# Gathering the inputs of four experts at a time instead of eight, with a fifth slot in a weight ring and layer-norm rows spread on the core

## The chip, the cores and the metric

The kernel runs on one core of a Trainium2 chip. The metric is the device time of one execution in microseconds (us). Where several runs are shown, their median is meant.

## The reference

One decoder layer on 256 tokens of width 1024. A mixer (gated linear attention and causal pooling) comes first, then a layer norm, then a mixture of 64 experts of which every token uses 8, then a second layer norm. The part that the change touches is the mixture:

```python
def expert_block(args):
    xb, gb = args
    h = (jax.nn.silu(jnp.einsum('td,edf->tef', xb, w_exp_gate))
         * jnp.einsum('td,edf->tef', xb, w_exp_up))
    return jnp.einsum('tef,efd->td', h * gb[..., None], w_exp_down)
...
x <- LayerNorm(alpha * x + mix(x))        # first norm, rows ln1_g and ln1_b
x <- LayerNorm(alpha * x + moe(x))        # second norm
```

Each expert has three float32 matrices of 1 MB: gate and up (1024 x 256) and down (256 x 1024). All 64 experts are read, 192 MB.

## The kernel before, in words

**Weights.** All weight loads stand in one list, in the order of use, and `Ring` (L52) issues them on SyncE's queue, one tile of 1 MB (128 partitions x 8 KB) each. The tiles lie in slots: ring1 has 8, ring2 has 6, ring3 has 4 (`NR1, NR2, NR3`, L23), and two more take the place of the transposed input (xTh, xTl). A slot takes the next load of the list as soon as its last reader is done (`done`, L104). Ring3 is opened at L808, late in the mixer's output stage, in memory that the mixer has given back. It takes no new load after q = 4 and is released at q = 7, where the shared expert's tensors take its place.

**Gathered inputs.** Each expert has 32 slots (CAP) for each of two token tiles of 128. `build_p` (L882) writes, for a token tile, a 0/1 matrix P8 of 128 tokens x (8 experts x 32 slots) with one VectorE instruction. `gather` (L889) multiplies it with the normed input, which is held as the sum of two float32r tensors, xh and xl. For each of 8 channel groups k there are four matmuls (xh and xl of two token tiles), each with 128 x 128 weights of its own and 256 moving columns (L899). One PSUM bank holds the result of one k, and `affine` (L769 to L773) applies the norm's gain and offset while it is copied to SBUF, odd k on VectorE, even k on ScalarE. The copy, xg, holds eight experts, 16 KB of each partition.

**The expert loop** (L1177) takes four experts per step q, 16 steps. The order of TensorE's work in a step is written out: `gate_up` of the first pair, the transposes of the hidden layer (`hidden_t`), the scatter of finished outputs (`flush`), `slot_gates` (two matmuls with P8 as weights and 8 columns), `build_pt`, half of the down products of the step before (`downs`), `gate_up` of the second pair, transposes, scatter, then at odd q the gather for the next eight experts (`gather(q // 2 + 1)`, L1235), then the other half of the down products. The first gather is at L934, ahead of the loop. At q = 10 the shared expert's up product (L832, tile w_sh_up, which stands in the list behind the second pair of q = 10) is placed between `slot_gates` and `build_pt`, at q = 11 its down product (L965).

**Rows of the first norm.** `residual` (L969) adds the normed input to the output sums, by quarters c of the channels, at q = 2 to 5 (`RES`). For it `load_rows` (L984) loads a quarter of ln1_g and of ln1_b, each copied by the DMA to all 128 partitions (128 KB written each), for c = 0 and 1 at q = 0 and for c = 2 and 3 at q = 3 and 4 (`ROWS`).

Of the kernel before, what the change touches and what calls it, by code (L numbers as in the profile page):

```python
# [5 lines left out]
FT = mybir.dt.float32  # L6
FR = mybir.dt.float32r
# [3 lines left out]
OP = mybir.AluOpType  # L11
# [4 lines left out]
E, FF, CAP = 64, 256, 32  # L16
# [3 lines left out]
NEG = -1e30  # L20
SPLIT1, SPLIT2 = 2, 3

NR1, NR2, NR3 = 8, 6, 4  # L23
LENT = ("up", 3)
CLOSE3, SH_X2, SH_UP, SH_DOWN, TAIL = 7, 8, 10, 11, 12
ROWS, RES = {0: (0, 1), 3: (2,), 4: (3,)}, {2: 0, 3: 1, 4: 2, 5: 3}

C_ID, C_MASK, C_TRI, C_IOTA, C_RC, C_SLOT, C_OWN = 0, 128, 320, 448, 480, 544, 545
C_COLS = 549
# [80 lines left out]
def body(ctx, tc, A, out, dbg=lambda *a: None, stop=None):  # L110
    nc = tc.nc
    ctx.enter_context(tc.manual_schedule())
    PE, V, S, G = nc.tensor, nc.vector, nc.scalar, nc.gpsimd
# [81 lines left out]
    def bank(tag, shape, name):  # L195
        t = psum.tile([128, 512], FT, name=name, tag=tag, bufs=4)
        n = 1
        for s in shape:
            n *= s
        v = t[:, :n]  # L200
        if len(shape) == 2:
            v = v.rearrange("p (a b) -> p a b", b=shape[1])
        elif len(shape) == 3:
            v = v.rearrange("p (a b c) -> p a b c", b=shape[1], c=shape[2])
        return v
# [3 lines left out]
    iota = cst[:, C_IOTA:C_IOTA + CAP]  # L209
# [11 lines left out]
    R1 = keep.tile([128, 2, E], FT, name="R1")  # L221
# [29 lines left out]
    for n in range(2):  # L251
# [12 lines left out]
                                     ap=[[0, 128], [1, E]]))  # L264
# [53 lines left out]
    p = bank("a", (128,), "warm")  # L318
# [450 lines left out]
    def affine(k, dst, p, on_vector):  # L769
        if on_vector:  # L770
            V.tensor_scalar(dst, p, g1T[:, k:k + 1], b1T[:, k:k + 1], op0=OP.mult, op1=OP.add)  # L771
        else:
            S.activation(dst, p, AF.Identity, bias=b1T[:, k:k + 1], scale=g1T[:, k:k + 1])  # L773
# [21 lines left out]
    moe = tc.alloc_tile_pool(name="moe", bufs=1, reuse_waits="tile")  # L795
    xh = moe.tile([128, 2, 8, 128], FR, name="xh")
    xl = moe.tile([128, 2, 8, 128], FR, name="xl")
# [10 lines left out]
    ring3 = tc.alloc_tile_pool(name="ring3", bufs=NR3, reuse_waits="tile")  # L808
    ring.open(ring3, "w3", NR3)
    mid = tc.alloc_tile_pool(name="mid", bufs=1, reuse_waits="tile")  # L810
    early = moe.tile([128, 4096], FT, name="x2T", tag="xg", bufs=1)
    x2T = early[:, :8 * T].rearrange("p (k t) -> p k t", t=T)
    sc = mid.tile([128, 2, E], FT, name="sc")
    pscore = bank("a", (2, E), "pscore")
# [29 lines left out]
    mb, mr = mbr[:, 0], mbr[:, 1]  # L844
    sel = mid.tile([128, 2, E], FT, name="sel")
    selb = mid.tile([128, 2, E], BF, name="selb")
    P8 = {}

    def group_sums(t):

# [28 lines left out]
        PE.matmul(prank, trib, selb, start=True, stop=True)  # L879
        V.scalar_tensor_tensor(R1, prank, 1.0, selb, op0=OP.add, op1=OP.mult)  # L880

    def build_p(o, t):  # L882

        if t == 0:
            P8[o] = moe.tile([128, 2, 8, CAP], FR, name="P8", tag="P8", bufs=1)
        V.tensor_tensor(P8[o][:, t], iota[:, None, :].to_broadcast([128, 8, CAP]),
                        R1[:, t, 8 * o:8 * o + 8, None].to_broadcast([128, 8, CAP]), OP.is_equal)

    def gather(o, banks="b", at_once=1):  # L889


        parts = [(0, xh), (0, xl), (1, xh), (1, xl)]
        for k0 in range(0, 8, at_once):
            ks = range(k0, k0 + at_once)
            p = {k: bank(banks[k % len(banks)], (2, 8, CAP), "pgat") for k in ks}
            for some in (parts[:3], parts[3:]):
                for k in ks:
                    for t, part in some:
                        PE.matmul(p[k][:, t].rearrange("p e s -> p (e s)"), part[:, t, k],  # L899
                                  P8[o][:, t].rearrange("p e s -> p (e s)"), start=part is xh, stop=part is xl)  # L900
            for k in ks:
                affine(k, xg[:, k].rearrange("p e t s -> p t e s"), p[k], k % 2)

    G.tensor_copy(xh[:, 0], by_channel(0))
    G.tensor_sub(xl[:, 0], by_channel(0), xh[:, 0].bitcast(FT))
# [21 lines left out]
    S.activation(xh[:, 1], by_channel(1), AF.Copy)  # L927
    ring.issue(ring1, "w1", NR1)
    dbg("x2T", x2T)
    xg = moe.tile([128, 4096], FT, name="xg", tag="xg", bufs=1).rearrange("p (k e t s) -> p k e t s", e=8, t=2, s=CAP)  # L930
    for t in range(2):
        build_p(0, t)
    V.tensor_sub(xl[:, 1], by_channel(1), xh[:, 1].bitcast(FT))  # L933
# [48 lines left out]
    rows1 = {}  # L982

    def load_rows(c):  # L984

        for n in "gb":
            rows1[n, c] = rest.tile([128, 256], FT, name="row" + n, bufs=2)
            src = A["ln1_" + n]
            nc.sync.dma_start(rows1[n, c], bass.AP(tensor=src.tensor, offset=src.offset + 256 * c,
                                                   ap=[[0, 128], [1, 256]]))  # L990

    mid.release()
    rest = tc.alloc_tile_pool(name="rest", bufs=1, reuse_waits="tile")
    GS, PT, HT = {}, {}, {}

    def slot_gates(q):

        p = bank("b", (4, 4), "pgs")
        for t in range(2):
            lhsT = P8[q // 2][:, t, 4 * (q % 2):4 * (q % 2) + 4].rearrange("p e s -> p (e s)")  # L1000
            PE.matmul(p[:, 2 * t:2 * t + 2], lhsT, gates[:, t, :, 4 * q:4 * q + 4], start=True, stop=True)
        own = st1.rearrange("p t c n -> p (t c n)")[:, :16].rearrange("p (a b) -> p a b", b=4)
        GS[q] = moe.tile([128, 2], FT, name="gsl", bufs=2)
        V.tensor_mul(own, p, cst[:, None, C_OWN:C_OWN + 4].to_broadcast([128, 4, 4]))
        V.tensor_reduce(GS[q], own.rearrange("p (t h) e -> p t (h e)", t=2), axis=AX.X, op=OP.add)
# [12 lines left out]
    def gate_up(i):  # L1018
        p = bank("b", (2, FF), "pgu")
        for g, n in enumerate(("gate", "up")):  # L1020
            w = [ring.get(li[n, 2 * i + c]) for c in range(2)]
            for k in range(8):
                for c in range(2):
                    e = (2 * i + c) % 8
                    PE.matmul(p[64 * c:64 * c + 64, g], xg[:, k, e].rearrange("p t s -> p (t s)"),  # L1025
                              w[c][:, k], start=k == 0, stop=k == 7, tile_position=(0, 64 * c))
            for c in range(2):
                ring.done(li[n, 2 * i + c])
        sg = moe.tile([128, FF], FT, name="sg", tag="sg", bufs=1)
        h = moe.tile([128, FF], FT, name="h", tag="h", bufs=1)  # L1030
        S.activation(sg, p[:, 0], AF.Silu)  # L1031
        V.tensor_mul(h, sg, p[:, 1])  # L1032
        return h
# [127 lines left out]
    def flush(keep=0):  # L1161
        while len(ready) > keep:
            scatter(ready.pop(0))
# [12 lines left out]
    hb = None  # L1176
    for q in range(NQ):  # L1177
        last = q == NQ - 1
        for c in ROWS.get(q, ()):
            load_rows(c)  # L1180
        if q in RES:
            ready.append(residual(0, RES[q]))
        ha = gate_up(2 * q)
        if q:
            hidden_t(2 * q - 1, hb)
        flush()
        slot_gates(q)
        if q % 2 and not last:
            build_p(q // 2 + 1, 0)
            build_p(q // 2 + 1, 1)  # L1190
        if q in RES:
            ready.append(residual(1, RES[q]))
        if q == 7:
            rest.release()
        if q == CLOSE3 - 3:
            ring.closed.add("w3")
        if q == CLOSE3:
            ring3.release()
            overflow()
            shp = tc.alloc_tile_pool(name="shp", bufs=1, reuse_waits="tile")  # L1200
            SH["x2"] = shp.tile([128, 8, T], FT, name="x2")
            for t in range(2):
                SH[t] = shp.tile([128, 8, 128], FT, name=f"xn{t}")
                G.tensor_add(SH[t], xh[:, t].bitcast(FT), xl[:, t].bitcast(FT))
        if q == SH_X2:

            for t in range(2):
                to_x2(SH["x2"], transposes(SH[t]), t, (0, 1, 2, 3))
        if q == SH_UP:
            p = bank("b", (2, T), "shu")  # L1210
            shared_in("w_sh_up", p, SH["x2"], slice(0, T))
            ring.done(li["w_sh_up"])
            V.tensor_mul(SH["h"], SH["h"], p)
        if q == SH_DOWN:
            shared_down()
            shp.release()
        if q == TAIL:
            tail = tc.alloc_tile_pool(name="tail", bufs=1, reuse_waits="tile")
            lnr = tail.tile([1, 2, D], FT, name="lnr2")
            nc.sync.dma_start(lnr[:, 0], A["ln2_g"])  # L1220
            nc.sync.dma_start(lnr[:, 1], A["ln2_b"])
            g2 = tail.tile([128, D], FT, name="g2")
            b2 = tail.tile([128, D], FT, name="b2")
        if q == TAIL + 1:
            G.partition_broadcast(g2, lnr[:, 0])
            G.partition_broadcast(b2, lnr[:, 1])
        build_pt(q)
        cs = pieces_of(q - 1)
        if q and not last:
            downs(q - 1, cs[0])  # L1230
        hb = gate_up(2 * q + 1)
        hidden_t(2 * q, ha)
        flush()
        if q % 2 and not last:
            gather(q // 2 + 1)  # L1235
        if q and not last:
            downs(q - 1, cs[1])
            done_downs(q - 1)
# [12 lines left out]
    o = [tail.tile([128, D], FT, name=f"o{t}") for t in range(2)]  # L1251
# [54 lines left out]
```

## Time and profile before

| | us |
|---|---|
| median of three runs (712.38 to 715.11) | 714.49 |
| the profiled execution, its time | 714.68 |
| its span in the trace | 712.9 |
| TensorE busy | 675.9 |
| VectorE busy | 292.4 |
| ScalarE busy | 229.3 |

The span is what the trace shows from the first to the last instruction, and 1.8 us of the execution's time lie around it. A position in the trace is given as time from the start of the span. The mixer takes the first 218 us or so, the router and the first gather some 20 more, and the expert loop runs from 240 us to 700 us. Matmuls overlap in the engine: a row's duration is that of one from its start to its end, and the cost of a row of them is the distance between their starts.

### The profile page before, as it was taken

The page shows a single profiled execution, that of the slowest core. Times are in us where ns is not written, and L with a number is a line of the kernel's source. Part 1 is how long each engine was busy: PE and PEld are TensorE (multiplying, and loading weights), DVE is VectorE, ACT ScalarE, POOL GpSimd, SP SyncE. Part 2 cuts the span into 40 slices and gives each one's busy share as a digit, 9 for nine tenths or more (in the row PEclk, how much of TensorE's full clock was granted, in tenths as well). Part 3 has the DMA queues.
Part 4 walks back from the last instruction along what each step waited for, and adds up shares of the span by engine and source line. Part 5 has one row for each costly group of instructions (what it writes and reads, how often), then busy time and mean ns, then how long its engine had stood idle before and what let it go on. Part 6 is the DMA issues. An engine that isn't in the chain of part 4 may idle for free. (4 is left out here: it accounts for less than half of the span.)

```text
span 712.9 us, 13836 instructions
## 1 busy us (share of the span) xinstructions
PE 675.9 (95%) x6004; PEld 481.0 (67%) x6004; DVE 292.4 (41%) x480; ACT 229.3 (32%) x356; POOL 61.0 (9%) x51
## 2 busy tenths in 40 slices
PE   7999999999999799999999999997959999999993
PEld 7999999999999556556556546554544465565641
DVE  3589745946676313444444123311302131221126
ACT  3654645764444213123123113211201121121142
POOL 1053303600002000000000002000000000100001
PEclk8999999999999999999999999999979999999997
DMA  8995543499667699999999999999998999999981
GB/s 277 301 310 174 155 142 119 133 385 419 240 241 294 212 424 397 405 422 410 416 419 419 421 419 417 422 419 419 422 421 351 416 403 423 418 422 420 389 262 61
DMA packets 70068, 243.10 MB, mean 341 GB/s; under 512 B 7122, under 2 KB 41682, under 8 KB 46196
## 3 DMA queue, kind: packets, MB, share of 16 engines
q1 hardware_dynamic: 69860, 242.12, 87.1%
q8 instruction: 48, 0.79, 0.5%
q10 hardware_dynamic: 144, 0.07, 0.1%
q14 instruction: 16, 0.13, 0.1%
HBM read 241.11 MB, written 1.05 MB: 340 GB/s over the span
## 5 line engine op out<-in xcount | busy, mean ns | idle before, releaser
L1025 PE MATMUL pgu<-w,xg 128*64 128x256 f32 x1744 | 227.7, 385 | 8.0 <-DVE maxi L955 4.4
L1025 PEld LDWEIGHTS pgu<-w,xg 128*64 128x64 f32 x1744 | 141.8, 138 | 82.8 <-ACT Y L1055 10.1
L1050 PE MATMUL py<-w,ht 128*32 128x512 f32 (+1 forms) x1016 | 120.0, 558 | 0.4 <-ACT x L773 0.3
L287 DVE TENSOR_TENSOR sl<-w,sh 128x1024 fp32r<-128x1024 f32 (+1 forms) x63 | 80.3, 1281 | 43.8 <-ACT sh L286 43.6
L1032 DVE TENSOR_TENSOR h<-sg,pgu 128x256 f32<-128x256 f32 x32 | 13.5, 421 | 188.5 <-ACT sg L1031 157.8
L1056 DVE SCALAR_TENSOR_TENSOR Y<-py,gsl,Y 128x512 fp32r<-128x512 f32 (+1 forms) x70 | 48.9, 704 | 91.8 <-ACT Y L1055 91.8
L1055 ACT ACTIVATE Y<-py,gsl 128x512 fp32r<-128x512 f32 (+1 forms) x70 | 45.3, 650 | 120.7 <-PE py L1050 120.7
L290 PE MATMUL proj<-xTh,sh 128*128 128x256 f32 x288 | 83.8, 291 | 0.0
L292 PE MATMUL proj<-xTh,sl 128*128 128x256 f32 x288 | 82.1, 285 | 0.0
L291 PE MATMUL proj<-xTl,sh 128*128 128x256 f32 x288 | 81.7, 284 | 0.0
L1031 ACT ACTIVATE sg<-pgu 128x256 f32<-128x256 f32 x32 | 12.3, 385 | 200.8 <-PE pgu L1025 200.8
L286 ACT ACTIVATE sh<-w 128x1024 fp32r<-128x1024 f32 (+1 forms) x63 | 64.3, 1028 | 35.2 <-PE proj L292 13.4
L1050 PEld LDWEIGHTS py<-w,ht 128*32 128x32 f32 x1016 | 31.7, 109 | 47.5 <-issue 41.7
L290 PEld LDWEIGHTS proj<-xTh,sh 128*128 128x128 f32 x288 | 55.1, 191 | 0.6 <-issue 0.3
L291 PEld LDWEIGHTS proj<-xTl,sh 128*128 128x128 f32 x288 | 55.4, 192 | 0.1
L292 PEld LDWEIGHTS proj<-xTh,sl 128*128 128x128 f32 x288 | 54.9, 190 | 0.0
L1025 PE MATMUL pgu<-xTh,xg 128*64 128x256 f32 x208 | 47.7, 381 | 0.0
L1025 PEld LDWEIGHTS pgu<-xTh,xg 128*64 128x64 f32 x208 | 27.7, 137 | 16.6 <-DVE Y L1056 5.9
L1050 PE MATMUL py<-xTl,ht 128*32 128x512 f32 x80 | 36.2, 594 | 0.0
L771 DVE TENSOR_SCALAR xg<-pgat,cols_sb 128x512 f32<-128x512 f32 x32 | 25.7, 809 | 14.2 <-PE pgat L899 12.2
L899 PE MATMUL pgat<-P,xl 128*128 128x256 f32 x128 | 30.6, 283 | 0.5 <-DVE xl L933 0.5
L899 PE MATMUL pgat<-P,xh 128*128 128x256 f32 x128 | 30.4, 283 | 0.0
(269 smaller groups left out, 946.3 us busy)
## 6 DMA issues: line engine op xcount, KB each, us to landing
w<-in_w_exp_up SPq DMA_DIRECT2D x58, 1024.0 KB, 14.1
w<-in_w_exp_gate SPq DMA_DIRECT2D x51, 1024.0 KB, 15.0
w<-in_w_exp_down SPq DMA_DIRECT2D x51, 1024.0 KB, 19.7
w<-in_w_in SPq DMA_DIRECT2D x21, 1024.0 KB, 7.9
xTh<-in_w_exp_gate SPq DMA_DIRECT2D x9, 1024.0 KB, 15.9
w<-in_w_exp_down SPq DMA_DIRECT2D x22, 256.0 KB, 6.0
xTl<-in_w_exp_down SPq DMA_DIRECT2D x5, 1024.0 KB, 12.0
w<-in_w_gla_up SPq DMA_DIRECT2D x4, 1024.0 KB, 11.2
```

The costliest lines, as they stand in the source:

```text
L286: S.activation(hi, src, AF.Copy)
L287: eng.tensor_sub(lo, src, hi.bitcast(FT))
L290: PE.matmul(o, ah, bh, start=start, stop=False, skip_group_check=shared_bank)
L291: PE.matmul(o, ah, bl, start=False, stop=False, skip_group_check=shared_bank)
L292: PE.matmul(o, al, bh, start=False, stop=stop, skip_group_check=shared_bank)
L771: V.tensor_scalar(dst, p, g1T[:, k:k + 1], b1T[:, k:k + 1], op0=OP.mult, op1=OP.add)
L899: PE.matmul(p[k][:, t].rearrange("p e s -> p (e s)"), part[:, t, k], P8[o][:, t].rearrange("p e s -> p (e s)"), start=part is xh, stop=par ...
L1025: PE.matmul(p[64 * c:64 * c + 64, g], xg[:, k, e].rearrange("p t s -> p (t s)"), w[c][:, k], start=k == 0, stop=k == 7, tile_position=(0, ...
L1032: V.tensor_mul(h, sg, p[:, 1])
L1050: PE.matmul(p[32 * c:32 * c + 32], HT[2 * q + c // 2][:, j, c % 2, t], ring.get(li["down", 4 * q + c])[:, j, cs], start=j == 0, stop=j == ...
L1055: S.activation(hi, p, AF.Copy, scale=g)
L1056: V.scalar_tensor_tensor(lo, p, g, hi.bitcast(FT), op0=OP.mult, op1=OP.subtract)
```

## The change

Inputs are gathered for four experts, in every step q but the last, instead of for eight in every other one. P4 and xg are half as large. A gather still has 8 channel groups with four matmuls each, now with 128 moving columns; two channel groups share a PSUM bank. The memory given back goes to a fifth slot of ring3. The rows of the first norm are loaded onto one partition, for one quarter per step (q = 1 to 4), and GpSimd copies them to the other partitions with `partition_broadcast`.

```diff
-NR1, NR2, NR3 = 8, 6, 4
+NR1, NR2, NR3 = 8, 6, 5
-ROWS, RES = {0: (0, 1), 3: (2,), 4: (3,)}, {2: 0, 3: 1, 4: 2, 5: 3}
+ROWS, RES = {1: 0, 2: 1, 3: 2, 4: 3}, {2: 0, 3: 1, 4: 2, 5: 3}
...
-    early = moe.tile([128, 4096], FT, name="x2T", tag="xg", bufs=1)
+    early = moe.tile([128, 2048], FT, name="x2T", tag="xg", bufs=1)
...
-    def build_p(o, t):
+    def build_p(q, t):
         if t == 0:
-            P8[o] = moe.tile([128, 2, 8, CAP], FR, name="P8", tag="P8", bufs=1)
-        V.tensor_tensor(P8[o][:, t], iota[:, None, :].to_broadcast([128, 8, CAP]),
-                        R1[:, t, 8 * o:8 * o + 8, None].to_broadcast([128, 8, CAP]), OP.is_equal)
+            P4[q] = moe.tile([128, 2, 4, CAP], FR, name="P4", tag="P4", bufs=1)
+        V.tensor_tensor(P4[q][:, t], iota[:, None, :].to_broadcast([128, 4, CAP]),
+                        R1[:, t, 4 * q:4 * q + 4, None].to_broadcast([128, 4, CAP]), OP.is_equal)
-    def gather(o, banks="b", at_once=1):
+    def gather(q, banks="b", at_once=1):
         parts = [(0, xh), (0, xl), (1, xh), (1, xl)]
-        for k0 in range(0, 8, at_once):
-            ks = range(k0, k0 + at_once)
-            p = {k: bank(banks[k % len(banks)], (2, 8, CAP), "pgat") for k in ks}
+        rhs = [P4[q][:, t].rearrange("p e s -> p (e s)") for t in range(2)]
+        for k0 in range(0, 8, 2 * at_once):
+            ks = range(k0, k0 + 2 * at_once)
+            p = {k // 2: bank(banks[k // 2 % len(banks)], (2, 2, 4 * CAP), "pgat") for k in ks[::2]}
             for some in (parts[:3], parts[3:]):
                 for k in ks:
                     for t, part in some:
-                        PE.matmul(p[k][:, t].rearrange("p e s -> p (e s)"), part[:, t, k],
-                                  P8[o][:, t].rearrange("p e s -> p (e s)"), start=part is xh, stop=part is xl)
+                        PE.matmul(p[k // 2][:, k % 2, t], part[:, t, k], rhs[t], stop=part is xl,
+                                  start=k % 2 == 0 and t == 0 and part is xh, skip_group_check=True)
             for k in ks:
-                affine(k, xg[:, k].rearrange("p e t s -> p t e s"), p[k], k % 2)
+                affine(k, xg[:, k].rearrange("p e t s -> p t e s"),
+                       p[k // 2][:, k % 2].rearrange("p t (e s) -> p t e s", s=CAP), k % 2)
...
     def load_rows(c):
-        for n in "gb":
-            rows1[n, c] = rest.tile([128, 256], FT, name="row" + n, bufs=2)
-            src = A["ln1_" + n]
-            nc.sync.dma_start(rows1[n, c], bass.AP(tensor=src.tensor, offset=src.offset + 256 * c,
-                                                   ap=[[0, 128], [1, 256]]))
+        rows1["one"] = rest.tile([1, 2, 256], FT, name="rowone")
+        for i, n in enumerate("gb"):
+            nc.sync.dma_start(rows1["one"][:, i], A["ln1_" + n][:, 256 * c:256 * (c + 1)])
+
+    def spread_rows(c):
+        for i, n in enumerate("gb"):
+            rows1[n, c] = rest.tile([128, 256], FT, name="row" + n)
+            G.partition_broadcast(rows1[n, c], rows1["one"][:, i])
...
     for q in range(NQ):
-        for c in ROWS.get(q, ()):
-            load_rows(c)
+        if q in ROWS:
+            load_rows(ROWS[q])
...
-        if q % 2 and not last:
-            build_p(q // 2 + 1, 0)
-            build_p(q // 2 + 1, 1)
+        if not last:
+            build_p(q + 1, 0)
+            build_p(q + 1, 1)
...
         hidden_t(2 * q, ha)
         flush()
-        if q % 2 and not last:
-            gather(q // 2 + 1)
+        if q in ROWS:
+            spread_rows(ROWS[q])
+        if not last:
+            gather(q + 1)
```

`slot_gates` and `gate_up` read P4[q] and expert e % 4 of xg accordingly.

## Rows read from the trace of the kernel before

**Rows 1.** The page: busy time by engine; TensorE's granted clock (tenths) in 40 slices.

```profile
PE 675.9 (95%) x6004; PEld 481.0 (67%) x6004; DVE 292.4 (41%) x480; ACT 229.3 (32%) x356; POOL 61.0 (9%) x51
PEclk8999999999999999999999999999979999999997
```

**Rows 2.** Busy time by stretch; the columns stand in the first line.

```profile
core 0: us, PE busy (x) PEld busy (x) DVE busy (x) ACT busy (x) POOL busy (x), PEclk, DMA share, GB/s
283.00:286.00 3.00, 3.00 (x30) 1.43 (x24) 1.69 (x3) 0.92 (x2) 0.00 (x0) 1.00 0.71 227
286.00:480.00 194.00, 192.29 (x1683) 112.04 (x1679) 65.75 (x122) 47.83 (x86) 4.73 (x2) 1.00 1.01 418
515.00:535.00 20.00, 9.98 (x47) 8.00 (x49) 0.62 (x3) 0.00 (x0) 0.00 (x0) 0.74 1.01 421
535.00:700.00 165.00, 164.41 (x1466) 90.91 (x1458) 40.06 (x75) 36.92 (x66) 2.48 (x2) 1.00 0.95 378
```

**Rows 3.** Timeline of PE, 480 to 535: start, us, work, [idle before, releaser].

```profile
480.33 4.64 PE L1050 MATMUL py<-w,ht 128*32 128x512 f32 x32
...
492.82 5.11 PE L1025 MATMUL pgu<-w,xg 128*64 128x256 f32 x30 [2.81 <-DMA w<-in_w_exp_up]
497.86 0.50 PE L1039 MATMUL pht<-cst,h 128*128 128x128 f32 x2
...
525.24 9.45 PE L832 MATMUL shu<-x,w 128*128 128x256 f32 x32 [10.02 <-DMA w<-in_w_sh_up]
```

**Rows 4.** The chain that ended last, where nothing waits: start, us, work.

```profile
437.62 3.82 PE pgat L899 x32
441.44 3.57 PE py L1050 x32
445.02 7.06 PE pgu L1025 x64
```

**Rows 5.** Runs of matmuls whose weights change each time, few columns: timelines, groups.

```profile
248.67 0.30 PEld L1001 LDWEIGHTS pgs<-gates,P 128*128 128x128 f32 x2 [0.39 <-issue]
...
L1001 PEld LDWEIGHTS pgs<-gates,P x32: 186/188/201, 248.7 to 670.0; 128*128 128x128 f32 x32
...
453.42 1.86 PE L778 MATMUL xp<-cst,xn 128*128 128x128 f32 x15
...
L778 PE MATMUL xp<-cst,xn 128*128 128x128 f32 x16 | 2.0, 276 | 0.0
...
225.39 4.01 PE L832 MATMUL shg<-x2T,w 128*128 128x128 f32 x34
```

**Rows 6.** Groups by line and shape: busy us, mean ns, idle before.

```profile
L771 DVE TENSOR_SCALAR xg<-pgat,cols_sb 128x512 f32<-128x512 f32 x32 | 25.7, 809 | 14.2 <-PE pgat L899 12.2
L1016 DVE TENSOR_SCALAR PT<-ppt,cst 128x256 fp32r<-128x256 f32 x16 | 7.7, 479 | 6.7 <-PE ppt L1013 6.7
L1225 POOL PARTITION_BROADCAST g<-lnr x1 | 1.3, 1302 | 163.7 <-DMA lnr<-in_ln_b 163.7
```

**Rows 7.** Timelines of DVE and PE ahead of the expert loop.

```profile
235.33 1.53 DVE L771 TENSOR_SCALAR xg<-pgat,cols_sb 128x512 f32<-128x512 f32 x2 [0.38 <-PE pgat L899]
236.77 0.22 DVE L936 CAST R1b<-R 128x128 bf16<-128x128 f32 x1
...
234.89 0.64 PE L899 MATMUL pgat<-P,xl 128*128 128x256 f32 x4
...
240.10 5.18 PE L1025 MATMUL pgu<-w,xg 128*64 128x256 f32 x32 [4.43 <-DVE maxi L955]
```

**Rows 8.** Timeline of SyncE's queue: the issues of weight loads and rows.

```profile
232.89 0.33 SPq L83 DMA_DIRECT2D w<-in_w_exp_gate  x1
240.29 0.34 SPq L989 DMA_DIRECT2D rowg<-in_ln_g  x1
...
245.29 0.33 SPq L83 DMA_DIRECT2D w<-in_w_exp_gate  x1
...
284.21 1.99 SPq L83 DMA_DIRECT2D w<-in_w_exp_down  x4
...
311.62 0.38 SPq L989 DMA_DIRECT2D rowg<-in_ln_g  x1
```

More of the change, by code (lines that the diff above doesn't have):

```diff
@@ L846, in body @@
     selb = mid.tile([128, 2, E], BF, name="selb")
-    P8 = {}
+    P4 = {}
     def group_sums(t):
@@ L929, in body @@
     dbg("x2T", x2T)
-    xg = moe.tile([128, 4096], FT, name="xg", tag="xg", bufs=1).rearrange("p (k e t s) -> p k e t s", e=8, t=2, s=CAP)
+    xg = moe.tile([128, 2048], FT, name="xg", tag="xg", bufs=1).rearrange("p (k e t s) -> p k e t s", e=4, t=2, s=CAP)
     for t in range(2):
@@ L999, in slot_gates @@
         for t in range(2):
-            lhsT = P8[q // 2][:, t, 4 * (q % 2):4 * (q % 2) + 4].rearrange("p e s -> p (e s)")
+            lhsT = P4[q][:, t].rearrange("p e s -> p (e s)")
             PE.matmul(p[:, 2 * t:2 * t + 2], lhsT, gates[:, t, :, 4 * q:4 * q + 4], start=True, stop=True)
@@ L1023, in gate_up @@
                 for c in range(2):
-                    e = (2 * i + c) % 8
+                    e = (2 * i + c) % 4
                     PE.matmul(p[64 * c:64 * c + 64, g], xg[:, k, e].rearrange("p t s -> p (t s)"),
```

## The prediction

> **What bounds the kernel now.** First the busy shares: TensorE is busy 95% of the span and VectorE 41%, so TensorE and the weight stream are what to look at [rows 1]. Then the stretches: from 286 to 480 us the DMA engines are full at 418 GB/s, and TensorE has work in 192.3 of 194 us [rows 2]. Both are near their limit at once. A step q takes 12 tiles of 1 MB (12.58 MB), 30.1 us at 418 GB/s; TensorE's work in a step is some 24.4 us, and 3.8 us more where a gather falls. TensorE therefore eats up the tiles that were loaded ahead, and the chain and TensorE's timeline show where it catches up with the stream [rows 3, 4]. At 480.3 the down products take 4.6 us instead of 3.6. The gate and up products behind them run from 484.9 to 497.9, 13.0 us where 7.1 is the rule. At 515.2 TensorE stops for w_sh_up, which lands at 525.2, and after this idle time the shared product runs at a granted clock of 0.74 over the stretch (part of it at 1.2 GHz) and takes 9.45 us [rows 2, 3]. From 535 to 700 TensorE is busy in 164.4 of 165 us [rows 2]. So the end is set by the moment at which the shared product of q = 10 is done (534.7), and by TensorE's work behind it. Ahead of it there are 1.0 + 5.9 + 10.0 + 2.4 us of waits and slow clock in which more work could hide.
>
> **The gather's price.** Today 32 matmuls of 256 columns take 3.82 us, 0.119 us each [rows 4]. Afterwards a gather of four experts still has 32 matmuls, each with weights of its own, and 128 columns. The question is whether half the columns take half the time. No 128-column float32r matmul stands in the trace. The nearest rows say that the change of weights sets the pace: slot_gates has float32r weights of the same size and only 8 columns, and its two weight loads together take 0.30 us where one takes 0.19, so the second starts 0.11 us after the first [rows 5]. Transposes with 128 columns follow each other at (1.86 - 0.28) / 14 = 0.113 us [rows 5]. I take 0.112: 32 x 0.112 = 3.58 us for each gather, nearly the old price for half the experts. The bounds are 0.060 (time in proportion to columns, 1.91 us) and 2 x 0.113 (the two passes that plain float32 needs, after the 128-column shg row [rows 5], 7.2 us); the float32r rows lie close to 0.112, and I stay there.
>
> **The sum on TensorE.** The loop has 7 gathers now (q odd, to 13) and 15 afterwards (q = 0 to 14): 15 x 3.58 - 7 x 3.82 = +27.0 us. Ahead of the shared product it is 10 x 3.58 - 5 x 3.82 = +16.7, behind it 5 x 3.58 - 2 x 3.82 = +10.3.
>
> **The first gather.** It runs ahead of the loop in the same number of matmuls, but its copies out of PSUM are half as long. VectorE is in them until 236.8, though the last matmul is done at 235.5, and the loop waits for VectorE's router chain behind them, until 240.1 [rows 7]. A copy of 256 columns takes about 0.48 us against 0.81 [rows 6]. The matmuls end about 234.2, the copies about 234.8: the loop starts 2.0 us earlier (0 to 2.5).
>
> **What lies beside other work.** A gather's copies (per step 4 x 0.48 us on VectorE, as many on ScalarE) are covered by the 3.57 us of down products behind it [rows 4, 6]; only at q = 0 none stand there, and the next gate product waits for the first channel groups: +0.4 us (0 to 0.9). Without that cover it would be as much at each gather. build_p is twice as often half as long, on a VectorE with time to spare, behind slot_gates, which VectorE waits for anyway. The rows: GpSimd is idle there, a broadcast of 1024 columns took 1.30 us [rows 6], two of 256 columns stand behind the landing of 1 KB loads; residual reads them a step later. Queued behind a late residual on VectorE is the product h of the next gate_up, TensorE's transposes wait for that, and some 7 us of gate_up cover it; without cover up to 2.6 us in each of four steps. The single row tile makes SyncE's next row load, and the weights queued behind it, wait for the broadcast of a step earlier: nothing, unless a broadcast is late by most of a step.
>
> **The weight stream.** The fifth slot is filled while SyncE otherwise has nothing to issue (no weight load between 232.89 and 245.29 [rows 8]): 1.05 MB, 2.5 us at 418 GB/s. The rows of c = 0 and 1 lie in that same gap, so taking them out gives nothing; those of c = 2 and 3 (four loads of 128 KB, from 311.6 on) lie in the full stretch: 0.52 MB, 1.3 us [rows 2, 8]. Against it: at 283 to 286 the stream runs dry (227 GB/s), until the down products of q = 1 release tiles at 284.2 [rows 2, 8]. Those releases come later by the new gather of q = 0: -2.0 + 0.4 + 3.58 - (3.82 - 3.58) = +1.7 us. So w_sh_up lands 2.5 + 1.3 - 1.7 = 2.1 us earlier (0 to 5), at 523.1.
>
> **The sum.** Free of waits TensorE would reach the shared product at 515.2 - 6.9 (the two slow stretches) - 2.0 + 0.4 + 16.7 = 523.4. The weights are there at 523.1, so both meet and no idle time is left. At the full clock the product takes about as long as a gate_up, which has as many column steps, 7.06 us [rows 4]: done at 530.5 against 534.7, 4.2 us earlier. Behind it +10.3. Together **+6.1 us**: 714.68 + 6.1 = 720.8 for the profiled execution. That one lies 0.2 above the median of the runs, so **720.6**.
>
> **Rivals.** (1) *Time goes with columns*, 0.060 us a matmul, 1.91 us a gather. TensorE's total then grows by 2 us only, it waits for w_sh_up again, and the stream decides: the dry stretch at 283 shrinks, w_sh_up lands about 4 us earlier, the product again at the slow clock, so 4 us are won there; behind it 5 x 1.91 - 7.64 = +1.9. Result -2.1: 712.6, not slower. The turning point is 4 / 5 + 7.64 / 5 = 2.3 us a gather, 0.073 us a matmul. For it speaks only that the 256-column row is near its columns' time, against it the 8-column row. The Trainium skill, TensorE: Matmul & The Clock Gate, section Back-to-back issue gap, gives about 81 ns for a sustained stream of weight loads with 128-column matmuls, which speaks for this side; no run here shows it, and the 0.11 us of this trace's float32-sized weights stands against it. As an estimate from that page's figure, 2.6 us a gather would end at about 716.
> (2) *Short float32r matmuls cost two passes*: 7.2 us a gather. TensorE would reach the shared product at 515.2 - 6.9 - 2.0 + 0.4 + 10 x 7.2 - 19.1 = 559.6, and behind it is +28.4: in all some +60, 775. slot_gates' two matmuls have two load records and not four, which speaks against it [rows 5].
> (3) *The fifth slot does not do what it says*: its memory comes free late, the stream gains nothing from it. w_sh_up lands at 525.6, TensorE idles 2.2 us, the end moves by +8.3: 723.
> (4) *Extra waits at each gather*, because copies or the rows push VectorE: 0.4 us in 15 steps, +6 more: 727.
>
> **Chances and range.** Forecast (0.105 to 0.119 us a matmul, the stream 0 to 5 us earlier) 0.65, with 717.5 to 724; rival 1 with all that lies between 0.06 and 0.09 us 0.15, with 711 to 717; rival 2 0.05; rival 3 0.07; rival 4 0.08. From 713.5 to 727 about 0.8 is held. A measurement of this kernel can tell about 0.5%, 3.6 us, from no change. Above 718.1 lie most of the forecast's case (0.52) and rivals 2 to 4 (0.20); below 710.9 a small part of rival 1 (0.05); between them 0.23.
>
> **What would show it.** Right: 32 gather matmuls of 128 columns in about 3.6 us in every step; the loop's first product near 238; the stops at 484.9 and 515.2 gone or down to 1 or 2 us, TensorE's clock at 1.0 through the shared product; the stream at 418 GB/s throughout with a longer dry stretch near 284. Wrong: a gather near 2 us (rival 1) or 7 us (rival 2), a wait for w_sh_up of over 3 us, or TensorE waiting for a broadcast.

## The result and the profile after

The changed kernel takes 721.48 us (median of four runs, 721.09 to 721.79), the kernel before in the same comparison 714.78 us. The medians lie 6.7 us apart, where 720.6 us and +6.1 us were forecast. The ratio of the runs is 1.0112, with a 95% interval of 1.0091 to 1.0133, which is some 8 us (6.5 to 9.5); the medians alone give 1.0094. Either way the kernel is slower by more than the noise.

The page after the change, its busy line and TensorE's granted clock over 40 slices (compare [rows 1]):

```profile
PE 696.4 (97%) x6260; PEld 505.8 (70%) x6260; DVE 301.9 (42%) x528; ACT 240.0 (33%) x388; POOL 64.4 (9%) x59
PEclk9999999999999799999999999999999999999997
```

TensorE is busy 20.5 us longer. Its clock no longer dips in the slice from 517 to 535 us, as it did before; it now dips to 0.7 in the slice from 234 to 252 us, behind the first gather. The chain that ended last, from 508 to 544 us and at its end (start, us, work; compare [rows 4]):

```profile
508.71 3.52 PE pgat L900 x32
512.23 3.58 PE py L1055 x32
515.81 8.73 DMA xTh<-in_w_sh_up
524.54 0.14 issue
524.68 7.14 PE shu L832 x32
531.82 0.23 PE ppt L1018 x8
...
543.91 3.52 PE pgat L900 x32
...
706.37 1.04 PE py L1055 x16
```

A gather of four experts costs 3.52 us, where one of eight cost 3.82. The shared product runs at once at full speed (7.14 us) and is done at 531.8, 2.9 us earlier than before. The last matmul of the loop ends at 707.4, 175.6 us later. In the kernel before, the last row of the same kind stood at

```profile
699.26 1.04 PE py L1050 x16
```

so it ended at 700.3, 165.6 us behind its shared product. TensorE's timeline at the shared product (the idle time before it in brackets; compare [rows 3]):

```profile
524.68 7.14 PE L832 MATMUL shu<-x,xTh 128*128 128x256 f32 x32 [0.34 <-DMA xTh<-in_w_sh_up]
```

The 10.0 us of waiting have shrunk to 0.3, and from 480 to 515 us TensorE does not wait at all (35.00 of 35 us busy, clock 1.00).

### The profile page after: what moved, and what is told of

It is laid out like the page before. It is cut to its first block, busy times and chain, and to the rows that moved or that the text cites. A ratio compares the mean times of both kernels' runs of the same rounds, so it can differ in the third digit from the quotient of the medians.

```text
span 719.8 us, 14443 instructions
## 1 busy us (share of the span) xinstructions
PE 696.4 (97%) x6260; PEld 505.8 (70%) x6260; DVE 301.9 (42%) x528; ACT 240.0 (33%) x388; POOL 64.4 (9%) x59
## 5 line engine op out<-in xcount | busy, mean ns | idle before, releaser
L1030 PE MATMUL pgu<-w,xg 128*64 128x256 f32 x1904 | 224.0, 384 | 5.0 <-DVE maxi L957 5.0
L900 PE MATMUL pgat<-P,xl 128*128 128x128 f32 x256 | 53.9, 275 | 0.0
L771 DVE TENSOR_SCALAR xg<-pgat,cols_sb 128x256 f32<-128x256 f32 x64 | 34.5, 543 | 45.4 <-ACT xg L773 45.4
L900 PE MATMUL pgat<-P,xh 128*128 128x128 f32 x256 | 52.0, 272 | 0.0
L1055 PE MATMUL py<-xTh,ht 128*32 128x512 f32 (+1 forms) x128 | 51.7, 541 | 0.0
L773 ACT ACTIVATE xg<-pgat,cols_sb 128x256 f32<-128x256 f32 x64 | 35.8, 565 | 41.6 <-PE pgat L900 35.6
L900 PEld LDWEIGHTS pgat<-P,xl 128*128 128x128 f32 x256 | 43.7, 192 | 0.7
```

What stands on the lines that cost most here:

```text
L900: PE.matmul(p[k // 2][:, k % 2, t], part[:, t, k], rhs[t], stop=part is xl, start=k % 2 == 0 and t == 0 and part is xh, skip_group_check=True)
L1055: PE.matmul(p[32 * c:32 * c + 32], HT[2 * q + c // 2][:, j, c % 2, t], ring.get(li["down", 4 * q + c])[:, j, cs], start=j == 0, stop=j == ...
```

## Experiments

Each was timed beside the kernel before on one chip. Chips differ (the kernel before took 712.12 to 714.78 us), so the ratios are what to compare.

### Does the change of weights set the gather's pace?

**Every matmul cut in two halves of 64 columns.**

```diff
-                        PE.matmul(p[k // 2][:, k % 2, t], part[:, t, k], rhs[t], stop=part is xl,
...
+                        n = 4 * CAP if q == 0 else 2 * CAP
+                        for c0 in range(0, 4 * CAP, n):
+                            PE.matmul(p[k // 2][:, k % 2, t, c0:c0 + n], part[:, t, k], rhs[t][:, c0:c0 + n],
...
```

> The changed kernel, where each 128-column matmul of the gathers in the loop is cut into two of 64 columns with the same weights: twice the matmuls, the same columns, the same result. If the change of weights sets the pace (0.112 us a matmul), a gather takes 64 x 0.107 to 0.112 = 6.8 to 7.2 us instead of 3.5, 15 gathers are 50 to 55 us longer, and the time is about 773. If the columns set it, a gather stays near 3.5 us and the time near 721.5 (under 725).

Measured: 832.67 us, ratio 1.1693 (1.1668 to 1.1718). With the columns unchanged and the matmuls doubled the kernel is 111 us slower than the changed one, twice the 50 to 55 us that were expected if weights set the pace. A gather's first matmuls, its place in the chain, and two stretches around it (columns as in [rows 2]):

```profile
500.84 0.27 PE L902 MATMUL pgat<-P,xh 128*128 128x64 f32 x1
500.95 0.39 PE L902 MATMUL pgat<-P,xl 128*128 128x64 f32 x2
501.17 0.39 PE L902 MATMUL pgat<-P,xh 128*128 128x64 f32 x2
...
500.97 9.73 PE pgat L902 x64
510.70 5.82 PE py L1058 x32
...
502.00:504.00 2.00, 2.00 (x21) 2.00 (x20) 0.55 (x1) 0.56 (x1) 0.00 (x0) 1.00 0.99 414
508.00:510.00 2.00, 2.00 (x11) 2.00 (x11) 0.47 (x1) 0.00 (x0) 0.00 (x0) 0.50 1.02 426
```

It begins at the expected pace: matmuls of 64 columns start at 500.84, 500.95 (two of them) and 501.17, 0.11 us apart. So halving the columns again wins nothing, and rival 1 falls. What came on top, and was not expected, is the clock: within the gather the granted clock falls from 1.00 to 0.50 (1.2 GHz), a gather takes 8.0 to 10.8 us, and the down products behind this one 5.8 instead of 3.6. In the changed kernel itself the clock stays at 1.00 there.

**The low part left out.** In the loop's gathers xl is not multiplied, so the experts' inputs are the float32r rounding of the normed input: 16 matmuls for 32, the copies as they were.

```diff
-for some in (parts[:3], parts[3:]):
+for some in (parts[:3], parts[3:]) if q == 0 else (parts[::2],):
...
```

> The changed kernel, where the gathers in the loop leave out the low part xl of the normed input: 16 matmuls instead of 32, the same copies. If the gathers' matmuls are what the change added, TensorE has 15 x 1.76 = 26 us less, it waits for w_sh_up again (some 15 us, and the shared product at the slow clock), and what is left is 5 x 1.76 = 8.8 us less behind that product and 2.3 us more for the clock: 715, down to 712 if earlier releases bring the weight stream forward. If the copies out of PSUM or the rows are what the change added, it stays within 2 us of 721.5.

Measured: 708.51 us, ratio 0.9948 (0.9929 to 0.9967), faster than the kernel before. On the first comparison's scale (0.9948 x 714.78) that is 711.1, just below the lower end of what was expected, and 10 us from the second theory. A gather takes 1.74 us, and TensorE waits again:

```profile
518.64 9.00 PE L832 MATMUL shu<-x,xTh 128*128 128x256 f32 x32 [13.17 <-DMA xTh<-in_w_sh_up]
```

The copies, GpSimd's work and the slot are the same as in the changed kernel. The loss is TensorE's time in the gathers.

**The split in bfloat16.** The two tensors of the normed input, P4 and the split gates are bfloat16, which leaves 16 bits of mantissa for the experts' inputs, the residual and the gates.

```diff
-xh = moe.tile([128, 2, 8, 128], FR, name="xh")
-xl = moe.tile([128, 2, 8, 128], FR, name="xl")
+xh = moe.tile([128, 2, 8, 128], BF, name="xh")
+xl = moe.tile([128, 2, 8, 128], BF, name="xl")
...
-gates = keep.tile([128, 2, 2, E], FR, name="gates")
+gates = keep.tile([128, 2, 2, E], BF, name="gates")
...
-            P4[q] = moe.tile([128, 2, 4, CAP], FR, ...)
+            P4[q] = moe.tile([128, 2, 4, CAP], BF, ...)
...
```

> The changed kernel with the normed input split into two bfloat16 tensors instead of two float32r (P4 and the split gates are bfloat16 as well): as many matmuls of 128 columns, with weights of half the bytes. The inputs of the experts and the residual then hold 16 bits of mantissa instead of 22. If the load of 4-byte weights is what sets 0.112 us a matmul, the pace falls to 0.06 to 0.08 us, a gather to 1.9 to 2.6 us, TensorE waits for w_sh_up again, and the time is near that of the kernel without xl: 0.995 to 1.000 of the kernel before. If any change of weights takes 0.11 us, it stays at 1.011.

Measured: 705.6 us, ratio 0.9884 (0.9864 to 0.9905). The timeline and the chain:

```profile
571.53 0.23 PE L900 MATMUL pgat<-P,xh 128*128 128x128 bf16 x1
571.59 0.22 PE L900 MATMUL pgat<-P,xl 128*128 128x128 bf16 x1
571.65 0.27 PE L900 MATMUL pgat<-P,xh 128*128 128x128 bf16 x2
...
571.68 1.80 PE pgat L900 x32
...
517.90 8.80 PE L832 MATMUL shu<-x,xTh 128*128 128x256 f32 x32 [13.54 <-DMA xTh<-in_w_sh_up]
```

As many matmuls of as many columns now start 0.057 us apart, and a gather takes 1.80 us. A single weight load, in the changed kernel (first line; shortest, median and longest in ns) and here:

```profile
L900 PEld LDWEIGHTS pgat<-P,xh x256: 188/192/201, 229.0 to 664.7; 128*128 128x128 f32 x128
...
276.15 0.10 PEld L900 LDWEIGHTS <-xh 128*128 128x128 bf16 x1 [0.28 <-issue]
```

Its row is half as long, 0.10 us instead of 0.19. So 0.11 us goes with 128 x 128 weights of four bytes, not with any change of weights. The edit changes the type of both operands; that the weights set the pace, and not the columns of the other operand, rests on these rows and on the 64-column kernel, where half the float32r columns took the same 0.11 us. The kernel is faster than was expected (0.995 to 1.000): TensorE again waits for the stream, and w_sh_up lands earlier than in the kernel before (6.4 us, counted as in the table further down). Part of that is the rows, below.

### What the other parts are worth

**The changed kernel again**, on the chip of the rows alone and of the changed kernel's bfloat16 runs.

> The changed kernel once more, beside the three that follow, on their chip: 1.0112 times the kernel before, as in its first measurement (1.009 to 1.0135).

Measured: 720.88 us, ratio 1.0102 (1.008 to 1.0125).

**Four slots in ring3**, the rest as changed (`NR3 = 4`).

> The changed kernel with four slots in ring3 as before. If the stream and TensorE meet at the shared product, w_sh_up lands 2.5 us (1 MB at 418 GB/s) later, TensorE idles for about as long, and the time is 723.5 to 724.5. If TensorE alone sets the end, it stays within 1 us of 721.5.

Measured: 723.66 us, ratio 1.0157 (1.0134 to 1.018), against 1.0112 and 1.0102 with five slots. That is 0.45 to 0.55%, 3.2 to 3.9 us, where 2 to 3 were expected; the intervals just overlap or just miss each other, so an effect of the slot is likely rather than certain. The trace shows how it arises:

```profile
525.82 8.83 PE L832 MATMUL shu<-x,w 128*128 128x256 f32 x32 [2.13 <-DMA w<-in_w_sh_up]
526.00:535.00 9.00, 9.00 (x44) 7.18 (x47) 0.31 (x1) 0.00 (x0) 0.00 (x0) 0.81 1.01 419
```

TensorE waits 2.1 us, and the product runs at a mean clock of 0.81 and takes 8.83 us instead of 7.14. So of the loss 1.7 us are the clock. This execution had a wait of 2.1 us, the changed kernel's 0.3 and (in its second profile) 1.0. The span behind the router's rank product (the small matmul L879, ahead of the first gather) is 493.2 us here and 491.9 and 490.7 with five slots: by the traces the slot is worth 1.4 to 2.6 us.

**Both channel groups of a bank on one engine.**

```diff
-affine(k, ..., k % 2)
+affine(k, ..., k // 2 % 2)
```

> The changed kernel with both channel groups of a PSUM bank copied by the same engine (engines change from bank to bank), where now VectorE's copy waits for ScalarE's of the same bank. If the copies are covered by the down products, only the first gather gains: the loop starts 0.5 to 1 us earlier, 720.5 to 721.5 in all. If waits of the copies at each gather are part of the loss, it is 4 us or more faster.

Measured: 720.44 us, ratio 1.0119 (1.0097 to 1.0141), as the changed kernel. From the rank product to the loop's first product it takes 9.66 us instead of 10.08, a little less than was expected. The copies' waits at each gather are covered.

**The rows alone**, in the kernel before: `ROWS`, `load_rows` and `spread_rows` as changed, everything else as before.

```diff
-ROWS, RES = {0: (0, 1), 3: (2,), 4: (3,)}, {2: 0, 3: 1, 4: 2, 5: 3}
+ROWS, RES = {1: 0, 2: 1, 3: 2, 4: 3}, {2: 0, 3: 1, 4: 2, 5: 3}
...
```

> The kernel before with the rows alone changed: one quarter per step, loaded onto one partition and spread by GpSimd; gathers of eight experts, four slots in ring3. If rows are hidden work, only the 0.52 MB of the quarters 2 and 3 leave the full stretch: 0 to 1.3 us faster (ratio 0.998 to 1.000). If GpSimd's broadcasts hold up VectorE and with it TensorE, it is 1 us or more slower (over 1.0015).

Measured: 710.47 us, ratio 0.9956 (0.9939 to 0.9973): 3.1 us faster, more than was expected and clear of no change. It computes the same values in the same order as the kernel before, and beats both kernels. The shared product, and GpSimd's two broadcasts of a quarter:

```profile
522.92 8.82 PE L832 MATMUL shu<-x,w 128*128 128x256 f32 x32 [11.50 <-DMA w<-in_w_sh_up]
...
L993 POOL PARTITION_BROADCAST rowg<-rowone x4: 549/550/555, 265.1 to 356.4; - x4
```

Counted from the router's rank product (at 229.17 here and 229.43 in the kernel before), the shared product starts 2.1 us earlier (293.75 against 295.81) and is 0.6 us shorter, 2.7 us in all. For the stream I had counted 1.3.

### What a slot is worth where TensorE waits

**Bfloat16 and a sixth slot** in the changed kernel (`NR3 = 6`, with both channel groups of a bank on one engine).

> As the bfloat16 kernel, with the 8 KB that it frees given to a sixth slot of ring3, and both channel groups of a bank copied by one engine. With short gathers the stream sets the moment of the shared product, so a slot is worth 2.5 us: 0.991 to 0.997 of the kernel before. If TensorE still sets it (gathers not shorter), the slot gives nothing, 1.010.

Measured: 705.31 us, ratio 0.9875 (0.9852 to 0.9898), the same as without it within the intervals (0.9884). The slot did its work on the stream, as the shared product shows:

```profile
514.95 9.96 PE L832 MATMUL shu<-x,w 128*128 128x256 f32 x32 [11.10 <-DMA w<-in_w_sh_up]
```

Counted from the rank product (228.53 without the slot, 228.30 with it), it starts 2.7 us earlier (286.65 against 289.37); but it takes 9.96 us instead of 8.80, at a mean clock of 0.71 instead of 0.81, so it is done only 1.6 us earlier. Behind the product nothing is lost: the span ends 475.4 us behind the rank product instead of 477.0. The medians do not show these 1.6 us, since the profiled execution without the slot was the slowest of its four (707.3 us, the median 705.6).

**The kernel before in bfloat16**, gathers of eight experts, four slots.

> The kernel before (gathers of eight experts, 256 columns) with the normed input, P8 and the split gates in bfloat16, four slots in ring3: the experts' inputs and the residual hold 16 bits of mantissa. At 256 columns the columns set the pace, so a gather takes 32 x 0.107 to 0.110 = 3.4 to 3.5 us instead of 3.8; TensorE waits for w_sh_up anyway, and behind it only 2 x 0.3 us are won, with up to 1 us more ahead of the loop: 0.997 to 1.000 of the kernel before. If bfloat16 shortens something else (copies, router chain), it is faster than 0.996.

Measured: 711.12 us, ratio 0.9971 (0.9951 to 0.999). A gather takes 3.51 us instead of 3.82: at 256 columns the type of the weights matters little.

**The same with a fifth slot**, which costs no gathers here.

> The same with a fifth slot of ring3 in the 8 KB that the bfloat16 tensors free, so that the slot comes without more gathers. TensorE waits for w_sh_up here, so if a slot is 1 MB more ahead of the stream, w_sh_up lands 2.5 us earlier than in the same kernel with four slots and the time is 2 to 2.5 us (0.003) lower. If the stream's dry stretches eat the slot, as the changed kernel's landing time suggests, it is under 1 us.

Measured: 707.73 us, ratio 0.9931 (0.9906 to 0.9956), 3.4 us less than with four slots. Both profiles show TensorE waiting for w_sh_up, and the product starting at

```profile
523.36 9.12 PE L832 MATMUL shu<-x,w 128*128 128x256 f32 x32 [12.04 <-DMA w<-in_w_sh_up]
...
519.78 8.80 PE L832 MATMUL shu<-x,xTh 128*128 128x256 f32 x32 [11.98 <-DMA xTh<-in_w_sh_up]
```

with four slots (first line) and with five. The rank products stand at 227.95 and 227.62, so it is 3.2 us earlier, where 2.5 were expected. Where TensorE's work does not grow, a slot gives its megabyte (2.5 us of the stream) and, by these two profiles, a little more.

## Why the prediction was right

**The gather's price held.** 3.58 us were forecast for 32 matmuls of 128 columns from the two float32r weight loads of slot_gates and from the transposes [rows 5]; 3.52 were measured. The 64-column kernel shows the same 0.11 us at half the columns, and the bfloat16 kernel shows that it belongs to four-byte weights. The 81 ns of the Trainium skill (TensorE: Matmul & The Clock Gate, section Back-to-back issue gap), from which the prediction estimated an end near 716, are met by neither kind here: 0.11 us with float32r weights, 0.057 us with bfloat16 ones.

**The growth behind the shared product held.** +10.3 us were forecast, 175.6 - 165.6 = +10.0 were measured.

**The meeting at the shared product held, with errors in both terms and a tie between them that the prediction did not have.** The table counts from the router's rank product, since the mixer's end moved by 1.5 us between the two profiles (rank product at 229.43 before, 227.93 after) and by as much among kernels that are the same up to there.

| from the rank product, us | before | forecast | after | after, second profile |
|---|---|---|---|---|
| first product of the loop | 10.67 | 8.7 | 10.08 | 10.09 |
| slot_gates of q = 0 | 19.2 | 17.2 | 20.1 | 18.7 |
| TensorE ready for the shared product | 285.8 | 294.0 | 296.4 | 294.5 |
| the shared product starts | 295.8 | 294.0 | 296.75 | 295.5 |

- *The first gather* was forecast to bring 2.0 us and brought 0.6. The step that failed is "the copies [end] about 234.8". The copies of all channel groups wait for the last eight matmuls, since the gather works on all eight groups at once, and VectorE waits for ScalarE's copy of the same bank; so VectorE's four copies of 0.48 us all follow the matmuls instead of running beside them (ScalarE's begin 0.6 us before the matmuls end). Counted from the rank product the matmuls end as forecast (4.9 us, forecast 4.8), but VectorE's copies end 6.8 us behind it (234.76 in this trace), where 5.4 were forecast and 7.4 stood before:

```profile
232.85 1.91 DVE L771 TENSOR_SCALAR xg<-pgat,cols_sb 128x256 f32<-128x256 f32 x4 [1.79 <-ACT xg L773]
...
238.01 3.25 PE L1030 MATMUL pgu<-w,xg 128*64 128x256 f32 x14 [5.03 <-DVE maxi L957]
```

  TensorE, done earlier with its matmuls, idles 5.0 us instead of 4.4. In the profile shown its clock was at 0.50 from 235 to 244 us (first line below; in the second profile 0.64, in the kernel before 0.81), and the first gate_up with what follows took 10.0 us against 8.6 in both the kernel before and the changed kernel's second profile. That is the 1.4 us by which the two profiles differ at slot_gates.

```profile
235.00:244.00 9.00, 5.99 (x28) 3.75 (x30) 2.27 (x11) 1.08 (x2) 0.00 (x0) 0.50 0.29 120
...
235.00:244.00 9.00, 5.56 (x38) 3.84 (x40) 2.69 (x13) 1.51 (x2) 0.00 (x0) 0.64 0.34 142
...
235.00:244.00 9.00, 4.57 (x28) 3.02 (x28) 4.03 (x14) 3.33 (x4) 0.00 (x0) 0.81 0.54 175
```

- *The stream* was forecast to bring w_sh_up 2.1 us earlier and brought it 0.3 us earlier in one profile and 0.9 later in the other. The failing step is the loss by later releases, which the prediction counted in one dry stretch only (1.7 us). The rows were worth more than their 1.3 us (2.1, above). Against them stands a long stretch in which the stream waits for slots, because TensorE is now hardly faster than the stream (the changed kernel from 300 us on, then the kernel before and the one without xl):

```profile
300.00:350.00 50.00, 50.00 (x446) 31.51 (x440) 19.94 (x37) 12.99 (x24) 1.85 (x4) 1.00 1.01 421
350.00:480.00 130.00, 127.78 (x1125) 77.64 (x1124) 41.33 (x88) 33.11 (x64) 5.64 (x4) 1.00 1.00 411
...
350.00:480.00 130.00, 128.29 (x1115) 74.96 (x1111) 37.58 (x71) 30.87 (x57) 4.73 (x2) 1.00 1.01 419
...
350.00:480.00 130.00, 128.55 (x1130) 76.09 (x1130) 40.07 (x88) 33.73 (x68) 5.66 (x4) 1.00 1.01 420
```

  411 GB/s over 130 us, where the kernel before has 419, is 1.04 MB, 2.5 us of stream: as much as the slot gave. The second profile has 409. The kernel without xl has the same slots and rows and shorter gathers, and its stream does not fall behind (420).
- *The tie.* The prediction set the landing of w_sh_up and TensorE's arrival as two times of their own. In the changed kernel's chain above, the load of w_sh_up is issued at 515.81, the moment at which TensorE's down products free its slot, and lands 8.73 us later (9.38 in the second profile, 10.52 with four slots). In the kernel before it was issued long ahead of its use, and was under way for 18.41 us:

```profile
506.69 18.41 DMA w<-in_w_sh_up
```

  So the landing now moves with TensorE's own work. That a slot changes how much stands in front of this load would fit the 10.52 us against 8.73 and 9.38, but it was not shown.

Neither error moved the end much, for the stream and TensorE set it together: of two times that lie within 1 us the later counts. That the sum came out within 1 us of the measured median is in part luck. In the profile shown the shared product was done 2.9 us earlier than before, not 4.2, and 1.5 us of that come from a mixer that ended earlier in this execution; counted from the rank product it was done 1.4 us earlier, 2.6 in the second profile. From the rank product to the end of the span it is 483.5 us before, 491.9 and 490.7 after: +8.4 and +7.2, as the ratios say (1.0112 and 1.0102 are 8.0 and 7.3 us), where +6.1 were forecast. So the term that was too large is the gain ahead of the shared product.

**The rivals.** *Time goes with columns* (712.6, not slower) fell; but its world exists: with two-byte weights the gather costs 1.80 us, and the kernel is faster than the one before, by 8 us rather than 2. What I had mis-sized in it is the stream, 4 us earlier against 6.4 measured (289.4 against 295.8 from the rank product). *Two passes* fell with the 3.52 us. *The fifth slot without effect* (723) is not what was measured: without the slot the kernel is slower again, by 3.2 to 3.9 us after the ratios and 1.4 to 2.6 us after the traces. *Extra waits at each gather* fell with the engines exchanged (720.44).

## What to carry to other kernels

A matmul that gets fewer columns per change of weights can cost as much as before (here with four-byte weights, and not with two-byte ones); look in the trace for the distance between matmuls with the narrowest operands of the same type before halving a tile, and count matmuls, not columns. Where one engine's work and a transfer stream finish together, a gain on the stream (here a slot, a megabyte) is worth its price only if nothing is added to the engine: got without more gathers the slot was worth 3.4 us; got with them it put 26 us more gathers on TensorE (15 x 3.52 - 7 x 3.82), and the kernel lost 6.7 us in the end, though the rows gained 3. Small loads that repeat rows over all partitions take time from a full stream, and moving them to an idle engine gave 3.1 us by itself.

## What the runs showed of the hardware that was not expected

- The granted clock fell although TensorE was never idle: in the 64-column kernel it went from 1.00 to 0.50 in the gather, after matmuls of 64 columns with new four-byte weights each, and stayed there into the down products, which took 5.82 us instead of 3.58. In the changed kernel's gather at the same place it stayed at 1.00. Why it fell is open.
- With bfloat16 weights of the same 128 x 128 size and 128 columns the distance between matmuls is 0.057 us, half of the 0.11 us with float32r.
- Four loads of 128 KB that write one row to all partitions seem to cost the stream more than their bytes: these 0.52 MB in the full stretch were worth some 2 us (one profile of each kernel), against 1.25 us at 418 GB/s. From 300 to 350 us, where they lie, the DMA moves 416 GB/s with them and 420 with the rows alone changed.
